# A two-layer attention trunk: 1/rms at the turns through Ln and Exp on ScalarE, and constants in two loads

## Chip, cores and metric

One core of one Trainium2 chip runs the kernel. The metric is the device time of one execution in microseconds (us), smaller is better. Engines are called as in the profile: PE is TensorE (PEld its weight loads), DVE is VectorE, ACT is ScalarE, POOL is GpSimd, SP is SyncE, which issues the DMAs.

## What is computed

Two layers over x of 256 tokens by 1024 channels, f32. Each layer has a token mixer (native sparse attention and block-sparse attention side by side) and a SwiGLU block; each of the two starts with an RMS norm whose scale and shift come from a conditioning vector c. Cut to what matters here:

```python
def rms_norm(x, g, eps=1e-6):
    x32 = x.astype(jnp.float32)
    y = x32 * lax.rsqrt(jnp.mean(x32 * x32, axis=-1, keepdims=True) + eps)
    return y.astype(x.dtype) * g

for l in range(2):
    ada = jax.nn.silu(c) @ w_ada[l] + b_ada[l]
    sh_m, sc_m, g_m, sh_f, sc_f, g_f = jnp.split(ada[:, None, :], 6, axis=-1)
    h = rms_norm(x, norm_mix[l]) * (1.0 + sc_m) + sh_m
    ... = jnp.split(h @ w_in[l], split_at, axis=-1)        # q, k, v, gates
    ...                                                    # both attentions
    x = x + g_m * (merged @ w_out[l])
    h = rms_norm(x, norm_ffn[l]) * (1.0 + sc_f) + sh_f
    gt, up = jnp.split(h @ w_ffn_in[l], 2, axis=-1)
    x = x + g_f * ((jax.nn.silu(gt) * up) @ w_ffn_out[l])
```

## The kernel before

Tokens lie in two tiles of 128 rows (t = 0, 1). A product x·W in f32 is made of three faster passes: x and W are each split into a rounded part `hi` and a rest `lo` (`split_unit`, L665: `hi` is an ACT copy, `lo` a DVE subtraction), and `mm3` issues hi·hi, hi·lo, lo·hi. Weights come through `dma` (L462) into a few `raw` slots of 1 MB; a slot is free again when its `lo` is done. In the lead-in four of the eight blocks of w_in are multiplied whole in f32 (`WHOLE`, tiles `raw,hd`) and four split.

The order of instructions on every engine is written by a planner (`Program.order`, L232). It walks in time over a cost for each operation, gives an operation with several possible engines to the one that ends first after adding `BIAS` (L130), takes the operation with the highest rank when several are ready, and emits one fixed stream for each engine. On the chip each engine follows its stream and waits where an operand is late. A change of one cost or one bias can therefore change the order everywhere. `R.ahead()` and `R.boost` raise a rank.

There are four norms, three of them between two sub-layers, called turns below: turn A after layer 0's mixer (stage `0wout`, L1359), turn B after layer 0's SwiGLU (stage `0fout`, L1430), turn C after layer 1's mixer. The first norm belongs to the lead-in (`lead_in`, L886). At a turn, for each t: `resid` (L1375) multiplies the product by the gate and adds it to x (DVE, two halves), `h_rstd` (L723) sums the squares of the halves (tile `tmp<-x`, ACT L729 or DVE L731), adds the two sums (`ssx`, DVE), makes sum/D + eps (`rx`, DVE L405), and raises it to -1/2 on POOL (L720); `h_norm` (L737) scales x by it (ACT L741, DVE L742); then PE transposes four blocks at a time (L454, `ident,tmp`), and `h_chain_` applies scale and shift and splits into `hp`, which PE multiplies next. PE has matmuls of the other tile to do meanwhile: the products of t = 1 while t = 0 is normed (`OUT_TURNS`), and the next sub-layer's for t = 0 while t = 1 is normed.

In the lead-in SP issues c, x, then for each block k of w_ada a load `sa` and one of w_in `raw`; one load of constants, `vecs` (128 rows of 707 numbers), comes behind block 0. It holds norm gains, b_ada, the compression offsets, the positions, the rope frequencies `inv` and the head gains. DVE adds 1 to some of it (`vecs<-vecs`, L405), makes block 0's scale and shift (`mod_m`) from `sa` and `vecs`, ACT makes `hd` from it, and PE starts on `raw,hd`. `angles` (L858) makes the rope angles out of positions and `inv` by 13 small operations on POOL, then two sines on ACT (`sincos`) with more POOL work between them.

Of the kernel before, what the change touches and what calls it, by code (L numbers as in the profile page):

```python
# [11 lines left out]
AF = mybir.ActivationFunctionType  # L12
# [4 lines left out]
P = 128  # L17
# [82 lines left out]
def AP(x):  # L100
    return x.ap() if isinstance(x, Ref) else x
# [9 lines left out]
class Op:  # L111
    def __init__(self, no, alts, key):
        self.no, self.alts, self.key = no, alts, key
        self.preds, self.succs, self.acc, self.new = {}, [], [], []
        self.bytes = 0
        self.level = 0.0
        self.stage, self.first, self.boost = None, False, 0.0

    def rank(self, e):
        return self.level + self.boost + (FIRST if self.first and e != "PE" else 0.0)  # L120
# [1 line left out]

FIRST = 1000.0
LAT = {"PE": 0.24, "DVE": 0.09, "ACT": 0.09, "POOL": 0.2, "SP": 0.0, "Q": 0.0}
SIZE = {F32: 4, F32R: 4, BF16: 2, I32: 4}


class Program:
    WAIT = 1.0
    BIAS = {"DVE": 0.6, "POOL": 0.5}  # L130

    def __init__(self, nc):
        self.nc, self.ops, self.kinds, self.key, self.open, self.allvals = nc, [], {}, 0.0, None, []
# [98 lines left out]
    def order(self):  # L232
# [13 lines left out]
        out = []  # L246
        eps = {"PE": 0.08, "DVE": 0.05, "ACT": 0.05, "POOL": 0.05, "SP": 0.0, "Q": 0.0}
        ends = {}

        def place(op):  # L250
            t = 0.0
# [29 lines left out]
        while len(out) < len(self.ops):  # L281
            best = None
            per = {}
            while loads and loads[0] in issued:
                loads.popleft()
            for op in ready:
                if "SP" in op.alts and op.no != loads[0] and self.ops[loads[0]].stage == "lead":
                    continue
                pl = place(op)
                if pl is None:  # L290
                    continue
                for e, (c, _) in op.alts.items():
                    est = max(free[e], pl[0],
                              max((f if q == e else f + LAT[q] for f, q in rt[op.no].values()), default=0.0))
                    per.setdefault(e, []).append((est, op, pl[1], c))
            self.done, self.ready = out, ready
            assert per, "stuck"
            for e, cs in per.items():
                t0 = min(c[0] for c in cs)
                if e == "SP":  # L300
                    pick = min(cs, key=lambda c: (max(c[0], free[e] + 0.3), c[1].no))
                else:
                    pick = max((c for c in cs if c[0] <= t0 + eps[e]), key=lambda c: (c[1].rank(e), -c[1].no))
                    if pick[3] > 1.0 and e != "PE":

                        soon = [c for c in cs if c[0] < t0 + self.WAIT * pick[3]
                                and c[1].rank(e) > pick[1].rank(e) + 5.0]
                        if soon:
                            pick = min(soon, key=lambda c: (c[0], -c[1].rank(e)))
                if best is None or pick[0] < best[0]:  # L310
                    best = (pick[0], e, pick[1], pick[2], pick[3])
            t, e, op, picks, c = best
            if len(op.alts) > 1:

                done = {x: next(y[0] for y in per[x] if y[1] is op) + op.alts[x][0] for x in op.alts}
                e = min(done, key=lambda x: done[x] + self.BIAS.get(x, 0.0))
                c = op.alts[e][0]
                t = done[e] - c
            for v, s in zip(op.new, picks):
                v.kind.queue.popleft()  # L320
                v.slot, v.placed = s, True
                for cell in s.cells:
                    cell.busy = True
            if op.bytes:
                free[e] = t + c
                if e == "SP":
                    dma = max(dma, t + c + 0.5) + op.bytes / 385e3
                    end = dma + 2.0
                else:
                    end = t + c + 6.5  # L330
            else:
                free[e] = t + c
                end = t + c
            ends[op.no] = end
            for v in op.acc:
                v.left -= 1
                v.end = max(v.end, end + LAT[e])
                if v.left == 0:
                    for cell in v.slot.cells:
                        cell.busy, cell.free_at = False, v.end  # L340
            ready.remove(op)
            if e == "SP":
                issued.add(op.no)
            for s in op.succs:
                npred[s.no] -= 1
                rt[s.no][op.no] = (end, e if not op.bytes else "SP")
                if not npred[s.no]:
                    ready.append(s)
            out.append((t, e, op))
# [13 lines left out]
class Engines:  # L363
# [52 lines left out]
    def recip(self, out, a):  # L416
        self._vec(("DVE",), cols(out), True, lambda v: v.reciprocal(AP(out), AP(a)), [a], [out])

    def act(self, out, a, func, scale=None, bias=None, accum=None):
        kw, reads = {}, [a]  # L420
        c = (0.17 if self._psum(a) else 0.215) + cols(out) / 1200
        if scale is not None:
# [8 lines left out]
        if accum is not None:  # L431
            kw["accum_out"] = accum
            writes.append(accum)
            c += 0.2
        self.p.op({"ACT": (c, [lambda: self.nc.scalar.activation(AP(out), AP(a), func,  # L435
                                                                 **{k: AP(x) for k, x in kw.items()})])},
                  reads, writes)

    def evac(self, out, a):

# [42 lines left out]
def trunk_kernel(tc, pools, A):  # L483
# [78 lines left out]
    crow = const("crow", [P, D])  # L562
    x = [const(f"x{t}", [P, D]) for t in range(NT)]
    NV = 2 * L * KD + L * 6 * KD + L * 16
    vecs = const("vecs", [P, NV + 35 + 256 * L])
    posi = vecs.of("pos")[:, NV:NV + 3].bitcast(I32)
    inv = vecs.of("inv")[:, NV + 3:NV + 35]
    gvec = [vecs.of("g")[:, NV + 35 + 256 * l:NV + 35 + 256 * (l + 1)] for l in range(L)]
    normT = vecs.of("norm")[:, :2 * L * KD].rearrange("p (a l k) -> p a l k", a=2, l=L)
    bT = vecs.of("b")[:, 2 * L * KD:8 * L * KD].rearrange("p (l s k) -> p l s k", l=L, s=6)  # L570
    peT = vecs.of("pe")[:, 8 * L * KD:NV].rearrange("p (l j) -> p l j", l=L)
# [148 lines left out]
        E_.raw("POOL", 1.1 + 0.13 * n, lambda: nc.gpsimd.tensor_tensor(AP(r), AP(r), AP(mh), op=ALU.pow), [r, mhalf], [r])  # L720
        return r

    def h_rstd(t):  # L723
        xr = [temp(), temp()]
        s2 = small(2, "ssx2")
        ss = small(1, "ssx")
        for i in range(2):
            xi, si, xo = x[t].of(i)[:, i * 512:(i + 1) * 512], s2.of(i)[:, i:i + 1], xr[i]
            R.op({"ACT": (0.84, [(lambda o, a, b: lambda: nc.scalar.activation(AP(o), AP(a), AF.Square, accum_out=AP(b)))  # L729
# [1 line left out]
                  "DVE": (0.77, [(lambda o, a, b: lambda: nc.vector.scalar_tensor_tensor(  # L731
                      AP(o), AP(a), 1.0, AP(a), op0=ALU.mult, op1=ALU.mult, accum_out=AP(b)))(xo, xi, si)])},
                 [xi], [xo, si])
        tt(ss, s2[:, 0:1], s2[:, 1:2], ALU.add)
        return xr, rstd_of(ss, 1, 1.0 / D, EPS, "rx")

    def h_norm(t):  # L737
        xr, r = h_rstd(t)
        for i in range(2):
            xi, xo = x[t].of(i)[:, i * 512:(i + 1) * 512], xr[i]  # L740
            R.op({"ACT": (0.72, [(lambda o, a: lambda: nc.scalar.activation(AP(o), AP(a), AF.Copy, scale=AP(r)))(xo, xi)]),  # L741
# [144 lines left out]
    def lead_in(bs, h, W):  # L886
# [7 lines left out]
        def load(k):  # L894
# [3 lines left out]
            raws[k] = R.val("raw", lambda a: a[:, :NC0])  # L898
            dma(raws[k], W[k * P:(k + 1) * P, :NC0])

        load(0)
        dma(vecs, A["vecs"])
        for k in range(1, KD):
            load(k)
        with R.ahead():
            consts()
# [8 lines left out]
            act(crow.of(i)[:, i * 512:(i + 1) * 512], b, AF.Copy)  # L915
        for kind in (1, 4):
            ts(bT[:, :, kind], bT[:, :, kind], 1.0, None, ALU.add)
        xr = [h_norm(t) for t in range(NT)]
        xT = {}
        for q in range(4):  # L920
            b = R.val("s" if q < 2 else "t")
# [44 lines left out]
    def sublayer_mix(l, h):  # L966
# [397 lines left out]
        for kh in range(2):  # L1364
            for c in range(2):
                us[(c, kh)] = load_unit(WO[kh * 512:(kh + 1) * 512, c * 512:(c + 1) * 512], 4, 512, spare=True)
        for c, kh, t in OUT_TURNS:
            part(bs[(c, t)], mT[t], us[(c, kh)], 4 * kh, kh == 0, kh == 1)
        for t in range(NT):
# [15 lines left out]
    def sublayer_ffn(l, h):  # L1385
# [60 lines left out]
        for i, t, k, c in keys:  # L1446
            kk = 2 * i + k
            cs_ = slice(c * 512, (c + 1) * 512)
            mm3(bs[(t, c)], aT[t][kk], us[i].hi[:, k, cs_], us[i].lo[:, k, cs_], kk == 0, kk == KF - 1)
        hn = []  # L1450
        for t in range(NT):
            for c in range(2):
                resid(l, t, c, bs[(t, c)], ada[l]["g_f"])
# [58 lines left out]
```

## Time and profile before

| what | value |
|---|---|
| median of 3 runs | 848.64 us (848.53 to 852.99) |
| the profiled execution | 847.45 us, its span 845.70 us |
| granted TensorE clock over the span | 0.987 of full speed |
| DMA | 183.82 MB, mean 217 GB/s |
| `vecs` load | 353.5 KB, 8.9 us from issue to landing |
| chain that ended last, by engine | PE 80%, DVE 6%, DMA 6%, ACT 3%, issue 2%, POOL 1% |

The span is the time from the first to the last instruction of the profiled execution; the 1.75 us beside it lie around them. The chain that ended last is followed back from the last instruction, at each step to what released it. A row of the timeline gives start, length, engine, line, operation, out<-in, and in brackets how long the engine had stood idle and what ended it.

### The profile page before, as it was taken

How to read it: one execution, taken by the hardware profiler on the slowest of the kernel's cores; microseconds unless marked ns; L12 is line 12 of the kernel's file. 1: busy time of each engine (PE TensorE's matmuls, PEld its weight loads, DVE VectorE, ACT ScalarE, POOL GpSimd, SP SyncE). 2: the span in 40 equal slices, each digit the busy share in tenths (PEclk: the TensorE clock that was granted, in tenths of full speed). 3: DMA queues.
4: the chain of work that ended last, by engine and by line, in shares of the span. 5: the costliest groups of instructions: out<-in, count | busy, mean ns of one | idle time of the engine just before them, and what ended most of it. 6: DMA issues, size and time to landing. Idle time of an engine off the chain costs nothing.

```text
span 845.7 us, 10445 instructions
## 1 busy us (share of the span) xinstructions
PE 806.8 (95%) x3948; PEld 613.3 (73%) x3948; DVE 578.7 (68%) x1023; ACT 404.2 (48%) x640; POOL 73.7 (9%) x75
## 2 busy tenths in 40 slices
PE   6998999998989999999999879999999999999996
PEld 3666756763778887888878758766567788889885
DVE  7979777766896867776788878674477454365443
ACT  6345275751572444433474345677356533354331
POOL 5411600000010000000012213000001000000000
PEclk9998999999999999999999989999999999999999
DMA  9988364458958888888847765430373455446431
GB/s 362 401 294 285 126 205 165 137 194 312 335 198 291 270 326 306 303 295 332 322 149 218 279 208 190 140 110 1 100 265 133 130 213 198 157 153 245 154 144 50
DMA packets 75204, 183.82 MB, mean 217 GB/s; under 512 B 4113, under 2 KB 9233, under 8 KB 75154
## 3 DMA queue, kind: packets, MB, share of 16 engines
q1 hardware_dynamic: 75154, 183.16, 61.5%
q8 instruction: 31, 0.51, 0.2%
q14 instruction: 19, 0.16, 0.1%
HBM read 182.10 MB, written 1.05 MB: 217 GB/s over the span
## 4 chain that ended last, share of the span: by engine, by line
PE 80%; DVE 6%; DMA 6%; ACT 3%; issue 2%; POOL 1%; POOLq 0%; SPq 0%; DVEq 0%; ACTq 0%
PE bank L450 75%; PE bank L454 5%; DVE lo L387 2%; ACT hi L435 2%; DMA aw<-in_w_ada 1%; DVE tmp L387 1%; DMA raw<-in_w_out 1%; DMA vecs<-in_vecs 1%; DMA raw<-in_w_ffn_in 1%; POOL rx L720 1%; DMA raw<-in_w_in 1%; DVE x L387 1%; DVE aw L393 1%; POOL tmp L387 0%; DVE tmp L405 0%
## 5 line engine op out<-in xcount | busy, mean ns | idle before, releaser
L450 PE MATMUL bank<-hi,hp 128*128 128x512 f32 (+2 forms) x1296 | 408.0, 388 | 4.7 <-DVE tmp L387 2.4
L435 ACT ACTIVATE hi<-raw 128x2048 fp32r<-128x2048 f32 (+2 forms) x107 | 201.5, 1892 | 267.8 <-PE bank L450 204.5
L387 DVE TENSOR_TENSOR lo<-raw,hi 128x2048 fp32r<-128x2048 f32 (+2 forms) x107 | 240.4, 2266 | 126.7 <-ACT hi L435 125.6
L450 PEld LDWEIGHTS bank<-hi,hp 128*128 128x128 f32 x1296 | 240.7, 190 | 60.5 <-issue 5.9
L450 PE MATMUL bank<-lo,hp 128*128 128x512 f32 (+2 forms) x648 | 246.1, 380 | 2.5 <-DVE lo L387 2.5
L450 PEld LDWEIGHTS bank<-lo,hp 128*128 128x128 f32 x648 | 123.3, 190 | 27.7 <-DVE lo L387 3.9
L393 DVE SCALAR_TENSOR_TENSOR aw<-aw,crow 128x1024 f32<-128x1024 f32 x80 | 95.6, 1219 | 24.6 <-DMA aw<-in_w_ada 24.5
L450 PE MATMUL bank<-hi,aT 128*128 128x512 f32 x352 | 111.0, 391 | 0.0
L450 PEld LDWEIGHTS bank<-hi,aT 128*128 128x128 f32 x352 | 66.1, 188 | 13.4
L450 PE MATMUL bank<-lo,aT 128*128 128x512 f32 x176 | 68.7, 390 | 0.0
L450 PE MATMUL bank<-raw,yy 128*128 128x512 f32 x128 | 58.6, 598 | 2.7 <-DVE tmp L393 2.6
L450 PE MATMUL bank<-raw,hd 128*128 128x512 f32 (+1 forms) x112 | 51.1, 586 | 2.0 <-ACT hd L435 2.0
L720 POOL TENSOR_TENSOR rx<-rx,mhalf 128x1 f32<-128x1 f32 x8 | 12.3, 1536 | 466.9 <-DVE rx L405 463.1
L454 PE MATMUL bank<-ident,tmp 128*128 128x128 f32 x256 | 38.8, 284 | 8.0 <-ACT tmp L741 4.2
L454 PEld LDWEIGHTS bank<-ident,tmp 128*128 128x128 f32 x256 | 31.0, 146 | 19.1 <-ACT tmp L741 6.4
L399 DVE CUSTOM_DVE_ANT_0 at<-bank,maskf 128x128 f32<-128x128 f32 (+1 forms) x96 | 29.6, 352 | 22.0 <-PE bank L454 14.6
L450 PE MATMUL bank<-hi,mT 128*128 128x512 f32 x128 | 42.7, 402 | 0.0
L450 PEld LDWEIGHTS bank<-raw,yy 128*128 128x128 f32 x128 | 23.0, 190 | 26.9 <-issue 24.3
L450 PEld LDWEIGHTS bank<-lo,aT 128*128 128x128 f32 x176 | 33.1, 188 | 6.8 <-DVE lo L387 0.2
L435 ACT ACTIVATE at<-at,nb,rqa 128x128 f32<-128x128 f32 (+1 forms) x64 | 34.2, 536 | 4.3 <-DVE nb L393 4.3
L450 PEld LDWEIGHTS bank<-raw,hd 128*128 128x128 f32 x112 | 20.9, 196 | 19.5 <-issue 15.4
L435 ACT ACTIVATE tmp<-bank 128x512 f32<-128x512 f32 (+2 forms) x46 | 22.2, 519 | 18.9 <-PE bank L450 9.0
(172 smaller groups left out, 712.2 us busy)
## 6 DMA issues: line engine op xcount, KB each, us to landing
raw<-in_w_ffn_in SPq DMA_DIRECT2D x44, 1024.0 KB, 6.8
aw<-in_w_ada SPq DMA_DIRECT2D x80, 512.0 KB, 5.4
raw<-in_w_in SPq DMA_DIRECT2D x30, 1024.0 KB, 5.3
raw<-in_w_ffn_out SPq DMA_DIRECT2D x22, 1024.0 KB, 5.0
sa<-in_w_ada SPq DMA_DIRECT2D x8, 1024.0 KB, 10.5
raw<-in_w_out SPq DMA_DIRECT2D x8, 1024.0 KB, 6.1
raw<-in_w_in SPq DMA_DIRECT2D x8, 908.0 KB, 8.4
raw<-in_w_up_nsa SPq DMA_DIRECT2D x4, 1024.0 KB, 5.0
```

The lines of the kernel that those rows point to most:

```text
L387: self._vec(engs, cols(out), True, lambda v: v.tensor_tensor(AP(out), AP(a), AP(b), op=op), [a, b], [out])
L393: lambda v: v.scalar_tensor_tensor(AP(out), AP(a), AP(s), AP(b), op0=op0, op1=op1, **{k: AP(x) for k, x in kw.items()}),
L399: lambda v: v.tensor_tensor_reduce(AP(out), AP(a), AP(b), 1.0, init, op0, op1, AP(accum)),
L435: self.p.op({"ACT": (c, [lambda: self.nc.scalar.activation(AP(out), AP(a), func, **{k: AP(x) for k, x in kw.items()})])}, reads, writes)
L450: self.p.op({"PE": (cost, [lambda: self.nc.tensor.matmul(AP(out), AP(lhsT), AP(rhs), start=start, stop=stop)])}, [lhsT, rhs], [out])
L454: self.p.op({"PE": (0.109, [lambda: self.nc.tensor.transpose(AP(out), AP(a), AP(ident))])}, [a, ident], [out])
L720: E_.raw("POOL", 1.1 + 0.13 * n, lambda: nc.gpsimd.tensor_tensor(AP(r), AP(r), AP(mh), op=ALU.pow), [r, mhalf], [r])
```

## The change

Three edits. At the turns, 1/rms is exp(-ln(sum/D + eps)/2): `ts` makes b = sum of the first half/D + eps as soon as that half is there, ACT does Ln(sum of the second half/D + b) and Exp(-0.5 ·), and the DVE add, the second DVE step and the POOL power go. The lead-in keeps POOL's power but also loses one DVE step. `log_soon` puts a load of ACT's table with both functions ahead of each turn, at a rank above all others, free to go once the last gates (turns A and C) or the last SwiGLU piece (turn B) are written. The planner is told of table loads (1.28 each), and DVE's bias goes from 0.6 to 0.8. `vecs` (now 163 numbers a row) goes ahead of block 0's loads; `rows` (544 a row, `inv` and the head gains) follows block 1.

```diff
-    BIAS = {"DVE": 0.6, "POOL": 0.5}
+    BIAS = {"DVE": 0.8, "POOL": 0.5}
...
+            if op.loads is not None:
+                table = op.loads
+            if e == "ACT" and op.func is not None and op.func not in table:
+                table = next(x for x in TABLES if op.func in x)
+                t = max(t, free[e] + 1.28)
...
-    def h_rstd(t):
+    def h_rstd(t, log):
...
-        ss = small(1, "ssx")
+        b, r = small(1, "ssx"), small(1, "rx")
...
-        tt(ss, s2[:, 0:1], s2[:, 1:2], ALU.add)
-        return xr, rstd_of(ss, 1, 1.0 / D, EPS, "rx")
+            if i == 0:
+                ts(b, si, 1.0 / D, EPS, ALU.mult, ALU.add)
+        s1 = s2.of(1)[:, 1:2]
+        if log:
+            act(r, s1, AF.Ln, scale=1.0 / D, bias=b)
+            act(r, r, AF.Exp, scale=-0.5)
+        else:
+            ts(r, s1, 1.0 / D, b, ALU.mult, ALU.add)
+            E_.raw("POOL", 1.23, lambda: nc.gpsimd.tensor_tensor(AP(r), AP(r), AP(mhalf), op=ALU.pow), [r, mhalf], [r])
+        return xr, r
+
+    def log_soon(late):
+
+        R.boost = 1000.0
+        op = R.op({"ACT": (1.28, [lambda: nc.scalar.preload_act_table_set("natural_log_exp_and_others")])}, late, [])
+        op.loads = TABLES[3]
+        R.boost = 0.0
...
+        dma(vecs, A["vecs"])
         load(0)
-        dma(vecs, A["vecs"])
-        for k in range(1, KD):
+        load(1)
+        dma(rows, A["rows"])
+        for k in range(2, KD):
             load(k)
...
-        xr = [h_norm(t) for t in range(NT)]
+        xr = [h_norm(t, False) for t in range(NT)]
...
+        log_soon([yv, *tgv.values()])
         for c, kh, t in OUT_TURNS:
...
+        if l < L - 1:
+            log_soon(last)
```

## Rows read from the trace of the kernel before

**Rows 1.** Windows: width, busy us (count) of PE, PEld, DVE, ACT, POOL; clock.

```profile
15.00:55.00 40.00, 40.00 (x137) 25.02 (x136) 33.12 (x58) 15.75 (x23) 15.21 (x19) 0.96 0.92 362
224.00:248.00 24.00, 21.53 (x107) 17.40 (x105) 21.32 (x38) 14.81 (x26) 3.99 (x2) 1.00 0.57 196
425.00:443.00 18.00, 16.21 (x84) 12.28 (x83) 14.98 (x26) 13.38 (x24) 4.07 (x2) 1.00 0.40 129
636.00:660.00 24.00, 21.79 (x108) 17.64 (x107) 17.11 (x29) 16.11 (x30) 3.08 (x2) 1.00 0.39 132
```

**Rows 2.** Timeline of turn A: start us, us, engine, instruction, [idle before, releaser].

```profile
241.91 0.74 PE L450 MATMUL bank<-hi,hp 128*128 128x512 f32 x2 [0.84 <-DVE hp L387]
...
242.07 0.19 ACT L729 ACTIVATION_READ_ACCUMULATOR tmp<-x 128x1 f32 x1
...
242.79 2.53 POOL L720 TENSOR_TENSOR rx<-rx,mhalf 128x1 f32<-128x1 f32 x1 [9.27 <-DVE rx L405]
...
245.36 1.34 ACT L741 ACTIVATE tmp<-x,rx 128x512 f32<-128x512 f32 x2 [1.29 <-POOL rx L720]
...
246.14 0.66 PE L454 MATMUL bank<-ident,tmp 128*128 128x128 f32 x4 [1.62 <-ACT tmp L741]
```

**Rows 3.** Timeline of turn B, same columns.

```profile
426.55 0.19 ACT L729 ACTIVATION_READ_ACCUMULATOR tmp<-x 128x1 f32 x1
...
427.20 2.52 POOL L720 TENSOR_TENSOR rx<-rx,mhalf 128x1 f32<-128x1 f32 x1 [181.88 <-DVE rx L405]
...
429.75 1.34 ACT L741 ACTIVATE tmp<-x,rx 128x512 f32<-128x512 f32 x2 [1.73 <-POOL rx L720]
...
430.53 1.27 PE L454 MATMUL bank<-ident,tmp 128*128 128x128 f32 x8 [0.97 <-ACT tmp L741]
```

**Rows 4.** Timeline of turn C, same columns.

```profile
642.91 0.55 POOL L720 TENSOR_TENSOR rx<-rx,mhalf 128x1 f32<-128x1 f32 x1 [126.51 <-DVE rx L405]
...
656.73 0.66 PE L454 MATMUL bank<-ident,tmp 128*128 128x128 f32 x4 [1.62 <-ACT tmp L741]
```

**Rows 5.** Groups by line on ACT: count, busy us, mean ns, idle.

```profile
L435 ACT ACTIVATE hp<-bank,mod_f 128x128 fp32r<-128x128 f32 x8 | 3.4, 450 | 2.6 <-DVE tmp L405 2.6
...
L435 ACT ACTIVATE gates<-bank 128x24 f32<-128x24 f32 x4 | 0.8, 194 | 0.0
```

**Rows 6.** Timeline of ACT: a table load and its successor; ends of idle stretches.

```profile
204.20 1.91 ACT L435 ACTIVATE hi<-raw 128x2048 fp32r<-128x2048 f32 x1 [17.21 <-DMA raw<-in_w_out]
...
250.52 1.28 ACT L435 ACT_TABLE_LOAD   x1
...
251.82 0.60 ACT L435 ACTIVATE tmp<-bank 128x512 f32<-128x512 f32 x1
...
413.79 1.92 ACT L435 ACTIVATE hi<-raw 128x2048 fp32r<-128x2048 f32 x1 [5.78 <-PE bank L450]
...
449.40 1.92 ACT L435 ACTIVATE hi<-raw 128x2048 fp32r<-128x2048 f32 x1 [3.13 <-PE bank L450]
...
614.11 1.91 ACT L435 ACTIVATE hi<-raw 128x2048 fp32r<-128x2048 f32 x1 [8.82 <-DMA raw<-in_w_out]
```

**Rows 7.** Timeline of the lead-in, same columns as turn A.

```profile
11.90 0.25 DVE L405 TENSOR_SCALAR vecs<-vecs 128x16 f32<-128x16 f32 x2 [1.20 <-DMA vecs<-in_vecs]
...
14.45 8.05 PE L450 MATMUL bank<-raw,hd 128*128 128x512 f32 x16 [2.04 <-ACT hd L435]
...
16.65 1.72 ACT L435 ACTIVATE hi<-raw 128x1816 fp32r<-128x1816 f32 x1 [1.80 <-DMA raw<-in_w_in]
...
24.11 0.28 ACT L435 ACTIVATE sincos<-tmp 128x96 f32<-128x96 f32 x1 [3.51 <-POOL tmp L405]
...
29.50 2.04 DVE L387 TENSOR_TENSOR lo<-raw,hi 128x1816 fp32r<-128x1816 f32 x1
...
32.12 0.40 PE L450 MATMUL bank<-lo,hp 128*128 128x512 f32 x1
```

**Rows 8.** Who waited for whom, PE from 443 to 636 us: total, times, longest.

```profile
PE bank L454 <- POOL tmp L387: 3.2, 1, 3.2
```

More of the change, by code (lines that the diff above doesn't have):

```diff
@@ L117, in __init__ @@
         self.stage, self.first, self.boost = None, False, 0.0
+        self.func, self.loads = None, None
     def rank(self, e):
@@ L124 @@
 LAT = {"PE": 0.24, "DVE": 0.09, "ACT": 0.09, "POOL": 0.2, "SP": 0.0, "Q": 0.0}
+TABLES = ((AF.Exp, AF.Tanh), (AF.Sin,), (AF.Silu, AF.Sin, AF.Tanh), (AF.Ln, AF.Exp))
 SIZE = {F32: 4, F32R: 4, BF16: 2, I32: 4}
@@ L248, in order @@
         ends = {}
+        table = ()
         def place(op):
@@ L417, in recip, with act @@
         self._vec(("DVE",), cols(out), True, lambda v: v.reciprocal(AP(out), AP(a)), [a], [out])
-    def act(self, out, a, func, scale=None, bias=None, accum=None):
+    def act(self, out, a, func, scale=None, bias=None, accum=None, late=()):
         kw, reads = {}, [a]
@@ L434, in act @@
             c += 0.2
-        self.p.op({"ACT": (c, [lambda: self.nc.scalar.activation(AP(out), AP(a), func,
-                                                                 **{k: AP(x) for k, x in kw.items()})])},
-                  reads, writes)
+        op = self.p.op({"ACT": (c, [lambda: self.nc.scalar.activation(AP(out), AP(a), func,
+                                                                      **{k: AP(x) for k, x in kw.items()})])},
+                       reads + list(late), writes)
+        if any(func in x for x in TABLES):
+            op.func = func
     def evac(self, out, a):
@@ L564, in trunk_kernel @@
     NV = 2 * L * KD + L * 6 * KD + L * 16
-    vecs = const("vecs", [P, NV + 35 + 256 * L])
+    vecs = const("vecs", [P, NV + 3])
+    rows = const("rows", [P, 32 + 256 * L])
     posi = vecs.of("pos")[:, NV:NV + 3].bitcast(I32)
-    inv = vecs.of("inv")[:, NV + 3:NV + 35]
-    gvec = [vecs.of("g")[:, NV + 35 + 256 * l:NV + 35 + 256 * (l + 1)] for l in range(L)]
+    inv = rows.of("inv")[:, :32]
+    gvec = [rows.of("g")[:, 32 + 256 * l:32 + 256 * (l + 1)] for l in range(L)]
     normT = vecs.of("norm")[:, :2 * L * KD].rearrange("p (a l k) -> p a l k", a=2, l=L)
@@ L733, in h_rstd, with h_norm @@
                  [xi], [xo, si])
[L734 to L738 removed]
+            if i == 0:
[13 more added lines that the diff above has]
+        R.boost = 0.0
+    def h_norm(t, log=True):
+        xr, r = h_rstd(t, log)
         for i in range(2):
@@ L1497 @@
     rows = np.concatenate([np.array(INV_FREQ, np.float32), gains.reshape(-1)])
-    host["vecs"] = np.concatenate([host["vecs"], spots.view(np.float32), np.repeat(rows[None], P, axis=0)], axis=1)
+    host["vecs"] = np.concatenate([host["vecs"], spots.view(np.float32)], axis=1)
+    host["rows"] = np.repeat(rows[None], P, axis=0)
     arrays, aps = {}, {}
```

## The prediction

> **What bounds the kernel now.** I read the page's busy times first: PE is busy nearly all the time, so a change gains only where PE stands still. The view of PE's waits and the windows by stage say where that is. In the lead-in PE stands until its first product of x starts at 14.45, and then runs without a gap from 15 to 55 [rows 1, 7]. The two big products after turns A and C run almost without a gap too. At the turns it stands: the windows show 24.00 - 21.53 = 2.47 us at turn A, 18.00 - 16.21 = 1.79 at B and 24.00 - 21.79 = 2.21 at C, 6.47 in all, at a granted clock of 1.00, the 2.4 GHz level [rows 1]. The chain of waits passes POOL's power in each turn. The rest, some waits in the two mixers and the tail, is touched only by a new order.
>
> The timelines show what ends each gap. At A's second tile the last sum of squares is there at 242.07 + 0.19 = 242.26, POOL's power runs from 242.79 for 2.53, ACT scales x at 245.36, and PE starts its transposes at 246.14 after standing 1.62 [rows 2]. At C the same gap is 1.62 [rows 4]. At B it is the first tile: sum at 426.74, POOL 427.20 for 2.52, ACT at 429.75, PE after 0.97 [rows 3]. So three gaps, 4.21 us, hang on the power. The power itself took 0.55 once [rows 4] and 2.52 to 2.53 where it stood beside a long DVE subtraction [rows 2, 3]: most of it is waiting, not arithmetic. The remaining 6.47 - 4.21 = 2.26 are later steps of the same chain: 0.85 at A behind a `hp` rest on DVE [rows 1, 2], 0.82 at B and 0.59 at C.
>
> **The turns.** From the last sum to the scaling it takes 3.10 us at A [rows 2] and 3.01 at B [rows 3]; this goes, with its three hand-overs between engines. In its place stand Ln and Exp of one column on ACT, which made the sum. No row has them. Bounds: a small activation without operand pointers took 194 ns, one of 128 columns with two pointers 450 [rows 5]. Ln has one pointer (b), Exp none, so both together cost 0.39 to 0.90; I take 0.5, nearer the 24-column row. b waits for DVE only by a step made while ACT squares the second half. So the chain shrinks by about 2.5, more than each gap, and the three close: 1.62 + 0.97 + 1.62 = 4.21. Below that they can stay open only if ACT is busy with something else (a rival). What is late next is the 2.26: the same `hp` chain arrives earlier, but DVE's residual adds for the other tile and the block-by-block hand-overs stay, and at C the first tile's power took only 0.55, so there is little to win. I take somewhat under half, 1.0 (bounds 0 and 2.26). The turns' sum is 5.2 (4.2 to 6.5). PE's matmuls afterwards follow without a gap, so a gain at a turn is kept.
>
> On ACT the edit adds Ln, Exp and table loads. A load took 1.28, and the next activation started 0.02 behind it [rows 6]. Three preloads are new; Silu was loaded after the turns already. Behind turn B the gates' Tanh of layer 1 now needs a load that it didn't need, and the load for Exp later in that layer goes. So the net is three loads, 3.85 us of ACT. I cost them at nothing, because ACT stood idle 17.21, 5.78 and 8.82 us just ahead of the turns and 3.13 behind the gates [rows 6]. Without that cover they cost up to 3.85.
>
> **The lead-in.** The wait of DVE for `vecs` was 1.20, and its two adds of 0.25 stood behind that [rows 7]; both were ahead of the step that makes `hd`, which ended PE's wait. With `vecs` first they are done before block 0 lands. Against that, 353.5 x 163/707 = 81.5 KB go ahead of block 0, some 0.25 us at the pace of the DMA in that stretch. PE starts 1.2 earlier. The moved DMA is one more issue of SP ahead of block 0, hidden by the 1 MB of x in flight.
>
> What it costs: `rows` lies behind block 1, so the bytes up to its end are those that stood up to the end of block 1's `raw` before, and that was there when ACT split it at 16.65 [rows 7]. The rope frequencies arrive 4.75 later than at 11.90. The 13 POOL steps then ended at 24.11, where ACT had stood 3.51 for them: 12.2 from the landing. If they take that again, ACT stands until 28.9, and the split of the fourth block queues behind it on ACT. Its rest on DVE began at 29.50 and ended at 31.54; PE's first use of a rest after that is at 32.12 [rows 7], so the slack is 0.58. A block of w_in also gets its slot from it, so a delay goes on to the end of the lead-in. Worst: the whole 4.75 goes on to that rest, and it ends 4.75 - 0.58 = 4.2 behind PE's use. Best: POOL runs faster, and all of the 1.2 stays. Between -1.2 and +4.2 I take 0: POOL's steps were long where DVE worked, and DVE soon stands idle when ACT does, so POOL should make up most of it; a point just over the middle of the worse side, 2.4, is a rival.
>
> The row behind that is the power's 0.55 against 2.53. The Trainium skill ("SBUF — State Buffer", "SBUF: two separate sides") says that DVE with two SBUF inputs and POOL exclude each other on a shared pair of ports for a whole instruction. By that rule the delay on POOL is DVE's work, in the lead-in too; the rows agree.
>
> **The order.** BIAS 0.8 moves work from DVE to ACT or POOL, and every engine's order is new. Its mean I take as 0. The nearest price is a residual: one add on POOL held PE for 3.2 [rows 8].
>
> **The sum.** On the profiled execution 847.45 - 5.2 = 842.2 (of it 1.75 outside the span). The median of the runs lies 1.19 above that execution, so the forecast is 848.64 - 5.2 = 843.4.
>
> **The rivals.**
> 1. The lead-in gains as well: everything closes, 848.64 - 6.47 - 1.2 = 841.0. For it: PE ran without a gap in the lead-in. Against: the slack of 0.58.
> 2. The rope angles block ACT: 848.64 - 5.2 + 2.4 = 845.8. For it: ACT already stood 3.51 there, and the landing moves by 4.75. Against: POOL's speed when DVE is idle. The Trainium skill's rule of the shared ports, named above, speaks for it.
> 3. The table loads come out on the path: 848.64 - 5.2 + 3.85 = 847.3. Against: the idle stretches [rows 6]. The Trainium skill ("ScalarE: Activation LUTs", "What ACT_TABLE_LOAD costs") has 2.66 us for a switch with its drain; by that figure the three would cost 8.0 and the time be 851.4. The row's 0.02 behind the load speaks against the drain.
> 4. The change doesn't do what it says: Ln waits on ACT behind a split of 1.9 at each turn. Then the chain is 2.4 instead of 3.1, it wins 0.7 at each of the three gaps, and the time is 848.64 - 2.1 = 846.5. For it: a split followed the square directly at A and C. Against: the turn's chain has the higher rank.
> 5. Slower: the higher bias puts more adds ahead of transposes on POOL, where a DVE subtraction holds them. At 3.2 each [rows 8] the gain of 5.2 is used up from the second on: two give 849.8, three 853.0. For it: this happened once. Against: the add costs POOL more in the plan than DVE even with 0.2 added.
>
> **How the numbers follow.** The measurement can tell 0.5%, 4.2 us, from no change: faster is below 844.4, slower above 852.9. Chances: the forecast 0.50 with its own range 841.5 to 846, rival 1 0.13, rival 2 0.18, rival 3 0.05, rival 4 0.05, rival 5 0.09. Below 844.4 lie four fifths of the forecast's half and all of rival 1: 0.53. Above 852.9 lies rival 5 with three adds or with rival 2 on top: 0.06. The rest, 0.41, is the same. The range of 8 in 10 goes from 840.2, just under rival 1, to 849.3, over rivals 2 to 4.
>
> **What would show it.** Right: PE's gaps of 1.62, 0.97 and 1.62 ahead of the transposes are gone, Ln and Exp stand directly behind the last square and take about 0.5, and the three preloads lie in ACT's idle stretches. In the lead-in PE starts near 13.2. `sincos` shows rival 2: if ACT stands for POOL beyond 27 and PE waits behind it for a DVE `lo`, the 1.2 is gone. Wrong would be gaps at the turns that only change their releaser, or new waits of PE in the mixers for POOL or DVE.

## The result, and the profile after

Measured in alternation with the kernel before, 20 executions of each, the changed kernel took 845.92 us (median; 842.91 to 849.25) against 850.61 (846.32 to 854.43): a ratio of 0.9948 with a 95% interval of 0.9933 to 0.9964, faster by 4.7 us. The forecast was 843.4 with a range from 840.2 to 849.3. So sign and time came out as forecast, but the sum behind them did not: the turns gave about a fifth of what was counted on them, and in the two profiles a term that I had set to zero gave the rest.

Executions of one kernel differ by several us, and the profiled one of after (848.27 us, span 846.5) is a long one, that of before (847.45, span 845.7) a short one. Their spans can't be set against each other. What can is TensorE's (PE's) idle time: span less PE's busy time. Of before it is 845.7 - 806.84 = 38.9 us, of after 846.5 - 811.88 = 34.6: less by 4.3, about what the medians say. The other side, the 5.0 us by which PE was busy longer with the same 3948 instructions, belongs to the one execution.

The windows of the kernel after (width, busy us and count of PE, PEld, DVE, ACT, POOL; clock, DMA share, GB/s). The first three are the turns; each begins 3 us ahead of the turn's first residual and is 24 us wide, which for the kernel before shows the same 2.47, 1.79 and 2.21 as [rows 1]. The last is the whole execution:

```profile
227.80:251.80 24.00, 22.63 (x108) 17.38 (x106) 20.84 (x35) 19.83 (x36) 0.00 (x0) 1.00 0.57 186
420.30:444.30 24.00, 20.83 (x95) 16.05 (x94) 19.30 (x36) 17.63 (x37) 0.00 (x0) 0.93 0.41 132
639.60:663.60 24.00, 23.14 (x110) 18.11 (x109) 18.17 (x30) 19.85 (x36) 0.00 (x0) 1.00 0.30 97
0.00:847.00 847.00, 811.88 (x3948) 615.95 (x3948) 576.18 (x1008) 418.29 (x668) 64.72 (x69) 0.99 0.62 217
```

POOL is gone from the turns. PE idles 1.37 at A, 3.17 at B and 0.86 at C: 5.40 us where it was 6.47. The turns gave 1.07, not 5.2. Outside the turns PE idles 34.6 - 5.4 = 29.2 us where it was 38.9 - 6.5 = 32.4: 3.2 us came from there.

Turn A's second tile, timeline of the kernel after (start us, us, engine, instruction, [idle before, releaser]), to be read beside [rows 2]:

```profile
243.97 0.19 ACT L741 ACTIVATION_READ_ACCUMULATOR tmp<-x 128x1 f32 x1
244.19 0.29 ACT L444 ACTIVATE rx<-ssx,ssx 128x1 f32<-128x1 f32 x1
...
244.52 0.20 ACT L444 ACTIVATE rx<-rx 128x1 f32<-128x1 f32 x1
244.75 1.34 ACT L768 ACTIVATE tmp<-x,rx 128x512 f32<-128x512 f32 x2
...
245.53 0.66 PE L465 MATMUL bank<-ident,tmp 128*128 128x128 f32 x4 [0.71 <-ACT tmp L768]
```

The chain is what the prediction said: Ln and Exp stand directly behind the last sum, and from the sum (244.16) to the scaling it takes 0.59 us instead of 3.10. But PE still stands 0.71 ahead of the transposes. At C the same gap is 0.73, and at B it is closed. What is left at A comes from PE's side. These are the windows from 3 us ahead of the turn's first residual to the end of PE's work ahead of the gap, in the kernel before and in the kernel after:

```profile
225.25:244.52 19.27, 18.42 (x88) 14.75 (x86) 16.59 (x32) 13.44 (x23) 3.19 (x2) 1.00 0.56 199
```

```profile
227.85:244.82 16.97, 16.81 (x79) 12.90 (x77) 14.15 (x27) 12.91 (x26) 0.00 (x0) 1.00 0.57 196
```

PE gets there 2.30 us sooner in the turn: 1.61 because the new order gives it less to do first (79 matmuls instead of 88), 0.69 because it idled less. The last sum comes 0.70 sooner (16.31 into the window instead of 17.01), and the chain behind it is 2.51 shorter: 1.62 - 0.70 - 2.51 + 2.30 = 0.71.

In place of its gap B has three others:

```profile
434.69 1.28 DVE L396 TENSOR_TENSOR x<-x,tmp 128x512 f32<-128x512 f32 x2
434.92 0.50 PE L461 MATMUL bank<-hi,hp 128*128 128x512 f32 x1 [0.76 <-ACT hp L444]
...
435.90 0.68 DVE L396 TENSOR_TENSOR hp<-tmp,hp 128x512 fp32r<-128x512 f32 x1
...
436.63 1.06 PE L461 MATMUL bank<-hi,hp 128*128 128x512 f32 x2 [0.98 <-DVE ssx L414]
...
441.86 1.31 DVE L396 TENSOR_TENSOR lo<-raw,hi 128x1120 fp32r<-128x1120 f32 x1
...
443.23 0.40 PE L461 MATMUL bank<-lo,hp 128*128 128x280 f32 x1 [1.43 <-DVE lo L396]
```

PE takes up the first tile sooner than before (its transposes start at 429.17, 8.85 into the window, instead of 10.20), uses up its first half, and then waits for the second half: its rest `hp` (435.90) stands on DVE behind the second tile's residual (434.69). The releaser named at 436.63 is the small step that follows `hp` on DVE; the operand is `hp`. The last gap is a `lo` of the weights that stands on DVE behind other work.

Outside the turns, two waits are shorter or gone. In the mixer of layer 0 the kernel before had this (PE's waits from 170 to 224 us: total, times, longest):

```profile
PE bank L450 <- DVE tmp L393: 2.6, 2, 1.7
PE bank L450 <- DVE lo L387: 0.3, 1, 0.3
```

and the kernel after this:

```profile
PE bank L461 <- DVE lo L396: 0.9, 1, 0.9
PE bank L461 <- ACT yy L453: 0.7, 1, 0.7
```

1.3 us less. At the opening of layer 1 the add on POOL of [rows 8] had held PE for 3.16. Three such adds of the rotary step stood on POOL there, and beside that wait the kernel before had these from 444 to 523 us:

```profile
PE bank L450 <- ACT vbd L435: 3.4, 1, 3.4
PE bank L450 <- DVE tmp L387: 2.4, 1, 2.4
```

In the kernel after the three adds are on DVE, and PE's waits in the same stretch are, but for one of 0.2,

```profile
PE bank L461 <- DVE tmp L396: 2.1, 1, 2.1
PE bank L461 <- ACT vbd L444: 1.7, 1, 1.7
PE bank L465 <- DVE kbd_tok L414: 1.5, 1, 1.5
PE bank L461 <- DVE lo L396: 1.4, 1, 1.4
```

7.07 us of idle time in that stretch where it was 9.06: 2.0 less. The wait for POOL went and the one for `vbd` halved, but two new waits for DVE took back 2.9. So 1.07 + 1.3 + 2.0 = 4.4 us account for the 4.3.

That is one pair of profiles. Of the kernels below, same_order and same_order2 have PE's old order and power_back the new one. From 150 us to turn A, where PE idled 2.85 before and 1.57 after, they show 2.14 and 2.66 against 1.74; in the 79 us behind turn B, 9.06 twice against 8.00. So the two shares are better read as 0.4 to 1.3 and 1.1 to 2.0.

### The profile page after: what moved, and what is told of

Read it like the earlier page. It is cut to its first block, busy times and chain, and to the rows that moved or that the text cites. A ratio compares the mean times of both kernels' runs of the same rounds, so it can differ in the third digit from the quotient of the medians.

```text
span 846.5 us, 10445 instructions
## 1 busy us (share of the span) xinstructions
PE 811.9 (96%) x3948; PEld 615.9 (73%) x3948; DVE 576.2 (68%) x1008; ACT 418.3 (49%) x668; POOL 64.7 (8%) x69
## 4 chain that ended last, share of the span: by engine, by line
PE 78%; DVE 8%; DMA 6%; ACT 4%; POOL 2%; issue 1%; SPq 0%; DVEq 0%; POOLq 0%; ACTq 0%
PE bank L461 73%; PE bank L465 5%; DVE lo L396 4%; DMA raw<-in_w_out 2%; ACT hi L444 2%; DMA rows<-in_rows 2%; DMA aw<-in_w_ada 1%; DVE tmp L396 1%; DMA raw<-in_w_ffn_in 1%; POOL tmp L396 1%; POOL tmp L414 1%; DVE tmp L414 1%; ACT hp L444 1%; DMA raw<-in_w_in 1%; DVE x L396 0%
## 5 line engine op out<-in xcount | busy, mean ns | idle before, releaser
L461 PE MATMUL bank<-lo,hp 128*128 128x512 f32 (+1 forms) x648 | 246.7, 381 | 4.6 <-DVE lo L396 4.5
L461 PEld LDWEIGHTS bank<-lo,aT 128*128 128x128 f32 x176 | 33.1, 188 | 6.7 <-DVE lo L396 0.2
L453 ACT ACTIVATE pt<-bank 128x512 f32<-128x512 f32 x35 | 20.8, 594 | 21.7 <-PE bank L465 21.7
L732 POOL TENSOR_TENSOR r<-r,mhalf 128x4 f32<-128x4 f32 x4 | 4.1, 1020 | 355.0 <-DVE r L414 355.0
```

The source lines that it names most:

```text
L453: self.p.op({"ACT": (0.17 + n / 1200, [lambda: self.nc.scalar.activation(AP(out), AP(a), AF.Copy)]), "DVE": (0.155 + n / 960, [lambda: sel ...
L461: self.p.op({"PE": (cost, [lambda: self.nc.tensor.matmul(AP(out), AP(lhsT), AP(rhs), start=start, stop=stop)])}, [lhsT, rhs], [out])
```

## The experiments

Theory one was the prediction's: the power in the turns costs what its three gaps show, and its removal brings that, in any order of the rest. Theory two: the gain needs the order that the planner makes for the changed kernel. All twelve kernels were timed in alternation with the kernel before. The table has PE's idle time from each profile and the ratio of times; the idle time leaves out what an execution takes longer in the same instructions.

| kernel | turns A + B + C | elsewhere | PE idle | ratio to before, 95% |
|---|---|---|---|---|
| before | 2.47 + 1.79 + 2.21 = 6.5 | 32.4 | 38.9 | |
| after | 1.37 + 3.17 + 0.86 = 5.4 | 29.2 | 34.6 | 0.9948 [0.9933, 0.9964] |
| same_order | 1.91 + 1.28 + 2.21 = 5.4 | 33.4 | 38.8 | 0.9992 [0.9968, 1.0016] |
| same_order2 | 1.75 + 1.23 + 1.71 = 4.7 | 35.3 | 40.0 | 0.9977 [0.9953, 1.0000] |
| turns_only | 1.39 + 2.98 + 0.87 = 5.2 | 36.5 | 41.8 | 1.0037 [1.0007, 1.0066] |
| loads_only | 2.48 + 1.80 + 2.27 = 6.6 | 33.9 | 40.4 | 1.0030 [1.0005, 1.0056] |
| bias_only | 2.57 + 1.80 + 2.22 = 6.6 | 33.1 | 39.7 | 1.0031 [1.0006, 1.0055] |
| loads_bias | 2.47 + 1.78 + 2.24 = 6.5 | 35.6 | 42.1 | 1.0040 [1.0016, 1.0065] |
| old_bias (turns, loads) | 1.39 + 2.99 + 1.13 = 5.5 | 32.8 | 38.3 | 1.0007 [0.9981, 1.0032] |
| no_loads (turns, bias) | 1.39 + 3.16 + 0.88 = 5.4 | 32.4 | 37.8 | 0.9976 [0.9956, 0.9996] |
| power_back | 4.71 + 5.17 + 4.69 = 14.6 | 30.2 | 44.8 | 1.0107 [1.0064, 1.0150] |
| vecs_behind | 1.33 + 3.18 + 0.87 = 5.4 | 37.6 | 42.9 | 1.0096 [1.0071, 1.0120] |
| bias7 | 1.31 + 2.99 + 0.88 = 5.2 | 30.9 | 36.1 | 0.9981 [0.9957, 1.0005] |
| tile0 | 2.47 + 3.22 + 1.84 = 7.5 | 30.0 | 37.5 | 0.9983 [0.9956, 1.0009] |

**same_order: the power away, the order kept.** Ln and Exp are issued behind the last square; the plan keeps the power's steps, with nothing issued for them, so that PE and SP run exactly the streams of before. A table preload is issued ahead of each turn, as in the change.

```diff
+        def tail():
+            ...
+            nc.vector.tensor_scalar(b, a[:, 0:1], 1.0 / D, EPS, op0=ALU.mult, op1=ALU.add)
+            nc.scalar.activation(AP(r), a[:, 1:2], AF.Ln, scale=1.0 / D, bias=b)
+            nc.scalar.activation(AP(r), AP(r), AF.Exp, scale=-0.5)
...
+        R.op({"POOL": (1.23, [lambda: None])}, [r, mhalf], [r])
```

> The kernel before with the power at the turns replaced by Ln and Exp on ACT (b on DVE, table preloads as in the change), while the planner still counts DVE's two steps and POOL's power: the streams of PE and SP stay instruction for instruction those of before. Theory 1 (the power's chain holds PE at the turns): PE's gaps of 1.62, 0.97 and 1.62 ahead of the transposes close, the later gaps of 2.26 stay for the most part, 3.5 to 4.5 us less than before. Theory 2 (the gain needs the new order, the chain is covered or waits for something else as soon as the power is gone): under 1.5 us less.

It gained nothing that can be told: 0.9992, and 1.07 us in the turns, as its second theory had it. Its turn A shows why:

```profile
239.82 0.18 ACT L742 ACTIVATION_READ_ACCUMULATOR tmp<-x 128x1 f32 x1
...
240.37 0.20 ACT L738 ACTIVATE rx<-rx 128x1 f32<-128x1 f32 x1
...
240.48 1.90 ACT L435 ACTIVATE hi<-raw 128x2048 fp32r<-128x2048 f32 x1
...
242.28 1.32 ACT L763 ACTIVATE tmp<-x,rx 128x512 f32<-128x512 f32 x2
243.04 0.66 PE L454 MATMUL bank<-ident,tmp 128*128 128x128 f32 x4 [0.62 <-ACT tmp L763]
```

The exponential is done at 240.57, but the scaling comes at 242.28: between them stands a split of 1.90, which in the kernel before had filled ACT's wait for the power. The planner had covered most of the power with it. Once the power is gone, the cover is the delay. The three gaps still fell to 0.62, 0 and 0.89, but PE's waits for the first tile's `hp`, 0.84 at A and 0.58 at C before, grew to 1.30 and 1.31.

**same_order2: the split out of the way.** The scaling of each tile's first half is issued behind the exponential:

```diff
             nc.scalar.activation(AP(r), AP(r), AF.Exp, scale=-0.5)
+            nc.scalar.activation(AP(xr[0]), AP(x[t].of(0)[:, :512]), AF.Copy, scale=AP(r))
```

> As same_order (TensorE's and SyncE's streams are those of the kernel before, the power is gone, logarithm and exponential stand on ScalarE), but the scaling of each tile's first half is issued on ScalarE directly behind the exponential, ahead of the evacuation (the split's first part, 1.9 us) that stood between the two in same_order. Theory one (rows 2 to 4: the three gaps of 1.62, 0.97 and 1.62 us hang on the way from the last sum of squares to the scaling, wherever the order comes from): the gaps close, TensorE idles some 4 us less in the three turns than in the kernel before, and the time falls by 3 to 4 us, ratio 0.995 to 0.997. Theory two (the gain needs the new order): the split that is now 0.7 us later holds TensorE as much as the scaling did before it, the turns keep an idle time of 5 us or more, and the ratio is 0.998 to 1.001.

The ratio was 0.9977, on the edge between the two. Turn A:

```profile
233.94 3.70 ACT L435 ACTIVATE hi<-raw 128x2048 fp32r<-128x2048 f32 x2
...
237.54 0.44 ACT L435 ACTIVATE hp<-bank,mod_f 128x128 fp32r<-128x128 f32 x1
...
243.69 0.73 PE L450 MATMUL bank<-hi,hp 128*128 128x512 f32 x2 [1.49 <-DVE hp L387]
...
244.46 0.72 ACT L739 ACTIVATE tmp<-x,rx 128x512 f32<-128x512 f32 x1
...
247.65 0.55 PE L454 MATMUL bank<-ident,tmp 128*128 128x128 f32 x3 [0.26 <-ACT tmp L768]
```

The three gaps of the power are now 0.26, 0 and 0.26 (1.62, 0.97 and 1.62 before): theory one was right on those, 3.7 of 4.2 us. But the wait for `hp` grew at A from 0.84 to 1.49 and at C from 0.58 to 1.45. That `hp` is the first tile's and stands ahead of the second tile's gap. At A the split that had filled ACT's wait for the first tile's power now runs behind the scaling, two splits in a row (233.94), and the first tile's evacuation starts 0.36 later than before: 8.10 us behind the turn's first residual (229.44) instead of 7.74. That is part of the 0.65. The work that covered one wait comes back in another. The turns kept 4.7 us, a net gain of 1.8, and the time fell by about 2.0 (0.9977). Its profile shows 2.9 us more idle time elsewhere, with PE's stream unchanged; the times don't show that, so single profiles scatter by that much outside the turns.

**Each part alone, and two at a time.** turns_only has the power replaced and the preloads in the plan, with the old load and the old preference of 0.6 for VectorE; loads_only and bias_only are the kernel before with that part; old_bias, no_loads and loads_bias leave one part out of the change. The edits are those of the change's diff, for instance

```diff
-    BIAS = {"DVE": 0.8, "POOL": 0.5}
+    BIAS = {"DVE": 0.6, "POOL": 0.5}
```

> The change's turns, preloads and planner rules, with the one load of constants and DVE's bias of 0.6 of before. Theory 1: the turns are the whole gain, 4 to 6 us less than before, as much as the whole change or a little more. Theory 2: less than 2.5 us, since the bias and the loads would bring the rest.

> The kernel before with only the constants in two loads, the small one ahead of block 0. Theory of the forecast: PE's first product about 1.2 us earlier, the rope angles later, together 0 (from -1.2 to +4.2). Rival, from the profile after the change (first product only 0.13 earlier, the compression products 2.5 later): the load ahead of block 0 delays block 0 by as much as it saves, and the kernel is 1 to 2.5 us slower than before.

> The kernel before with only DVE's bias at 0.8. Theory 1: a new order of mean 0, within 2 us of before. Theory 2: the bias takes work off DVE in the mixers and brings 2 us or more.

> The whole change but for the planner's preference for VectorE, which stays at 0.6: logarithm and exponential, table preloads, two loads. If the gain of the whole change is that of the turns' power (theory one), about 0.995 like the kernel after; if it comes only with the order that the higher preference gives (theory two), 1.000 to 1.005, as turns_only and loads_only gave.

> The whole change but for the loads: the constants come in one load behind w_ada's first block, as in the kernel before. Theory one: 0.995 or a little lower, since the two loads alone cost 0.3%. Theory two, in the form that the turns' gain needs the preference of 0.8: 0.995 too; in the form that it needs the loads as well: 1.000 to 1.004.

> The kernel before with the two loads and the preference of 0.8, and the power still on GpSimd in the turns: all of the change but its turns. Theory one: no gain, 1.000 to 1.006 (the two parts alone gave 1.003 each), so that the difference to the kernel after, some 0.8%, is what the turns give within this order. Theory two in its strongest form (the gain is one of order, not of the turns): 0.995 to 0.997.

Each part alone made the kernel slower by 0.3 to 0.4%, loads and bias together by 0.4%, all three together faster by 0.5%. Neither theory of turns_only had a loss in it, and the 2.6 us that bias_only lost lie outside both of its theories, though its interval reaches into the first. The 2.6 us of loads_only are what its rival said, but not for the rival's reason, since PE's first product started 0.33 earlier there (14.12). loads_bias came out by its first theory, old_bias by its second, and no_loads between its two. The parts don't add: the same turns are worth +0.4% on the kernel before, and -0.9% on loads_bias (0.9948 against 1.0040). The turns themselves can't be the reason, since of these kernels all with the change's turns idle 5.2 to 5.5 us there and all with the old ones 6.5 to 6.6. The difference lies elsewhere, from 29.2 to 36.5 us. Two waits in it can be tied to parts. PE's wait for the add on POOL at the opening of layer 1 is in all kernels whose plan has the power in the turns (before, same_order, same_order2, loads_only, bias_only, loads_bias: 3.2 each time) and in none whose plan has the logarithm. The wait in the mixer of layer 0 (2.6 in before) is 2.6 in turns_only, 2.3 in old_bias, 1.3 in no_loads, and gone where logarithm, two loads and a preference of 0.7 or more come together (after, bias7, tile0, power_back, vecs_behind). Of the 4.1 that turns_only lost elsewhere, 2.3 stand ahead of 100 us and the rest is spread. Why the planner's order comes out so was not followed further.

**bias7: half the preference.**

```diff
-    BIAS = {"DVE": 0.8, "POOL": 0.5}
+    BIAS = {"DVE": 0.7, "POOL": 0.5}
```

> The whole change with a preference for VectorE of 0.7, half way from 0.6 (1.0007) to 0.8 (0.9948). If the preference itself gives the gain, step by step: 0.997 to 0.999. If the orders are draws that share only the turns: the turns idle 5.2 to 5.6 us as in all kernels with the change's turns, and the ratio is anywhere from 0.995 to 1.002, following the idle time outside the turns.

0.9981, between 1.0007 (0.6) and 0.9948 (0.8), with the turns unchanged at 5.2. Three points in order speak for the first expectation; since the intervals of neighbours touch, the second isn't excluded.

**power_back: the order of after, with the power in it.** The reverse of same_order: the plan is that of the change, and its two steps issue VectorE's multiply-add and GpSimd's power. No table is preloaded in the turns.

```diff
-            act(r, s1, AF.Ln, scale=1.0 / D, bias=b)
-            act(r, r, AF.Exp, scale=-0.5)
+            # the plan's two steps on ScalarE issue the power's two steps
+            for step, func, kw in (
+                    (lambda: nc.vector.tensor_scalar(AP(r), AP(s1), 1.0 / D, AP(b), op0=ALU.mult, op1=ALU.add),
+                     AF.Ln, dict(a=s1, scale=1.0 / D, bias=b)),
+                    (lambda: nc.gpsimd.tensor_tensor(AP(r), AP(r), AP(mhalf), op=ALU.pow),
+                     AF.Exp, dict(a=r, scale=-0.5))):
+                act(r, func=func, **kw)
+                R.ops[-1].alts["ACT"] = (R.ops[-1].alts["ACT"][0], [step])
```

> The kernel after with its own order on every engine, but the two steps of the logarithm and the exponential issue the power again (VectorE's multiply and add, then GpSimd's power), and no table is preloaded in the turns. TensorE's and SyncE's streams are those of the kernel after. The three turns idle 5.4 us in the kernel after, 6.5 in the one before. Theory one (the gain of the whole change is mainly that of order elsewhere, since the turns differ by 1.1 us only): the ratio stays at 0.996 to 0.997, turns at 6.5 to 7. Theory two (the order of the kernel after leaves no work between the last sum of squares and the scaling, so that the power, back in it, is uncovered): scalings come 1.5 to 2.5 us later each, the turns idle 9 to 12 us, and the ratio is 0.999 to 1.003.

Theory two held here, and more strongly than expected: 1.0107, 1.6% above the kernel after, and 14.6 us of idle time in the turns, 9.2 more. Turn A, second tile:

```profile
242.36 2.29 DVE L396 TENSOR_TENSOR lo<-raw,hi 128x2048 fp32r<-128x2048 f32 x1
...
244.56 0.21 DVE L752 TENSOR_SCALAR rx<-ssx,ssx 128x1 f32<-128x1 f32 x1
244.85 0.55 POOL L754 TENSOR_TENSOR rx<-rx,mhalf 128x1 f32<-128x1 f32 x1 [10.61 <-DVE rx L752]
...
245.44 1.34 ACT L774 ACTIVATE tmp<-x,rx 128x512 f32<-128x512 f32 x2 [2.88 <-POOL rx L754]
...
246.21 1.57 PE L465 MATMUL bank<-ident,tmp 128*128 128x128 f32 x8 [3.01 <-ACT tmp L774]
```

The same subtraction in the kernel before, beside its power of 2.53 (242.79) [rows 2], as the first of two:

```profile
242.63 4.48 DVE L387 TENSOR_TENSOR lo<-raw,hi 128x2048 fp32r<-128x2048 f32 x2
```

The power takes 0.55 here, not 2.53, and from the last sum to the scaling it is 2.88 all the same, where it was 3.10 in the kernel before: the multiply-add ahead of the power stands on DVE behind the subtraction of 2.29. So at this tile the delay is that subtraction in both kernels. In the kernel before ACT had a split in that time and PE other matmuls; here ACT stands 2.88 and PE 3.01. Part of the 9.2 is the place where DVE's step was put, and it is no pure price of the power; but it is what two more hand-overs cost in an order that leaves them no room. Outside the turns it idles 30.2, close to the 29.2 of after, without the preloads: they cost nothing there that can be seen.

**vecs_behind: the small load behind block 0.**

```diff
-        dma(vecs, A["vecs"])
         load(0)
+        dma(vecs, A["vecs"])
         load(1)
```

> The whole change, but the small load stands behind the loads of block 0 and ahead of those of block 1. If the 81 KB ahead are what made block 0's w_ada part land 1.3 us later, it lands at some 9 us again, and VectorE waits for the small load instead, about 1 us, as in the kernel before; TensorE's first product then stays at 14.1 to 14.5 us and the time at 0.993 to 0.996, as the kernel after. If the planner's order, which the moved load shifts in 98 places of TensorE's stream, decides more than the load: 0.997 to 1.002, with the turns' idle time unchanged at 5.4 us.

1.0096, far off both expectations. Lead-in of vecs_behind, timeline and window:

```profile
11.01 0.25 DVE L414 TENSOR_SCALAR vecs<-vecs 128x16 f32<-128x16 f32 x2 [2.71 <-DMA vecs<-in_vecs]
...
13.19 1.22 DVE L402 SCALAR_TENSOR_TENSOR sa<-sa,crow 128x1024 f32<-128x1024 f32 x1
...
18.02 2.93 PE L461 MATMUL bank<-raw,hd 128*128 128x512 f32 x3 [5.48 <-ACT hd L444]
```

```profile
15.00:55.00 40.00, 36.57 (x120) 22.25 (x121) 30.36 (x57) 14.77 (x23) 16.80 (x22) 1.00 0.77 294
```

With the load behind block 0 the plan puts the adds on `vecs` ahead of the first dot product on DVE, so DVE stands 2.71 for them and the dot product, 10.20 in after, comes at 13.19; PE's first product comes at 18.02. Then the loads fall behind too (294 GB/s from 15 to 55 us), PE has gaps where it had none, and up to 100 us it idles 8 us more than in after. So what costs here is the place of the adds in DVE's order. In no_loads, where the one load also lies behind block 0, the dot product stands ahead of the adds on DVE, and PE's first product starts at 14.62. What the small load ahead is worth by itself this run doesn't show.

**tile0: the first tile ahead of the second.** An attempt at a better kernel: the first tile's chain gets a higher rank, to close the gaps that turn B now has.

```diff
-HBOOST = (20.0, 20.0)
+HBOOST = (40.0, 20.0)
```

> The whole change, with the first tile's chain ranked ahead of the second tile's (20 more) in the turns, so that in turn B the second tile's residual no longer stands on VectorE between the two halves of the first tile's evacuation (0.76 and 0.98 us of TensorE's idle time in the kernel after). Theory one: those 1.7 us close, the turns idle 3.5 to 4.5 us instead of 5.4, and the ratio is 0.992 to 0.994. Theory two (order elsewhere moves as well, 178 places of TensorE's stream): turn B's idle time falls, but the ratio is 0.995 to 1.001. Rival within the turn: the second tile is now late, and its wait takes over the 1.7 us.

The rival within the turn came true. PE's waits ahead of the second tile's transposes at A, and then two of its waits at B:

```profile
242.43 0.66 PE L465 MATMUL bank<-ident,tmp 128*128 128x128 f32 x4 [1.82 <-ACT tmp L768]
```

```profile
433.13 0.74 PE L461 MATMUL bank<-hi,hp 128*128 128x512 f32 x2 [0.38 <-DVE hp L396]
439.23 0.39 PE L461 MATMUL bank<-lo,hp 128*128 128x280 f32 x1 [1.99 <-DVE lo L396]
```

At B 0.98 became 0.38, and 1.43 became 1.99; at A and C the second tile waits 1.82 and 1.84 instead of 0.71 and 0.73. The turns idle 7.5 us, and nothing is won. No kernel of these is faster than the kernel after.

## Why the prediction was right or wrong

- **What bounds the kernel.** Right in sign: of the thirteen changed kernels only same_order2 (1.2 us more idle, 0.2% faster) and old_bias (0.6 less, 0.1% slower) have a ratio that doesn't go with PE's idle time. In size the two can differ: power_back and vecs_behind are 9.1 and 8.2 us slower than the kernel before with 5.9 and 4.1 more idle, and the rest of that isn't explained.
- **The chain of the turns.** Right to the number: Ln and Exp took 0.29 and 0.20 (forecast 0.5 together), and the chain shrank from 3.10 to 0.59, by 2.51 (forecast 2.5).
- **"More than each gap, and the three close: 4.21."** This step failed. Of the three gaps 0.71, 0 and 0.73 are left, so 2.77 closed. I read a gap as the amount by which the chain was late, in an order that stays, and took it that only other work on ACT could keep it open. In the kernel after ACT has none there, but PE reaches the gap sooner, at A with 1.61 us less work ahead of it. same_order and same_order2 show that an order that stays doesn't help either: work that had filled the wait now delays the chain (1.90 of a split) or the first tile's `hp`.
- **"What is late next ... 1.0 of 2.26."** The term that was mis-sized most. The later waits didn't shrink by 1.0 but grew from 2.26 to 5.40 - 1.44 = 3.96, by 1.7: from 0.82 to 3.17 at B, while A and C gave back 0.6. At B I had looked only at the first tile. Its bounds of 0 and 2.26 excluded a loss without a reason. The turns' sum is 1.07 instead of 5.2.
- **Table loads at nothing.** Right: preloads stand at 194.42, 419.52 and 606.19, in stretches in which PE doesn't wait for ACT; outside the turns power_back without them idles no less. The load itself, in the kernel after:

```profile
419.52 1.28 ACT L760 ACT_TABLE_LOAD   x1
420.82 1.09 ACT L453 ACTIVATE gbc<-bank 128x512 f32<-128x512 f32 x2
```

  The Trainium skill ("ScalarE: Activation LUTs", "What ACT_TABLE_LOAD costs") gives a switch with its drain 2.66. The trace differs, and it decides: the load takes 1.28 here and the next activation starts 0.02 behind it, as in [rows 6]. Rival 3 doesn't apply.
- **The lead-in at 0.** Right in the sum. Timeline of the kernel after:

```profile
7.07 0.25 DVE L414 TENSOR_SCALAR vecs<-vecs 128x16 f32<-128x16 f32 x2 [0.37 <-DMA vecs<-in_vecs]
...
10.20 1.23 DVE L402 SCALAR_TENSOR_TENSOR sa<-sa,crow 128x1024 f32<-128x1024 f32 x1 [1.02 <-DMA sa<-in_w_ada]
...
14.32 6.33 PE L461 MATMUL bank<-raw,hd 128*128 128x512 f32 x8 [1.62 <-ACT hd L444]
```

```profile
15.00:55.00 40.00, 39.94 (x132) 24.28 (x130) 32.06 (x55) 15.47 (x22) 17.60 (x22) 1.00 0.98 370
```

  `vecs` no longer holds DVE, but block 0 is 1.33 later in this profile (10.20 instead of 8.87) where I had 0.25 from the bytes, so PE starts 0.13 earlier here, not 1.2. This pair of profiles misleads. Over all profiles in which DVE waits for it, block 0 lands at 9.39 to 10.20 with the small load ahead (five, median 9.56) and at 8.87 to 10.21 without (five, median 9.04): by the medians some 0.5 of the 1.33 is the load, an estimate, since the two ranges overlap; the rest is scatter. PE's first product starts at 13.71 to 14.93 in the seven profiles with the small load ahead (median 13.93) and at 14.45 to 15.81 in the six with one load (median 14.95; vecs_behind, with its other order on DVE, left out): 1.0 earlier, near the forecast's 1.2. The sum is 0 all the same: up to 55 us PE idles 6.79 and 6.84 in the median of the same profiles. What it gains at its start it loses in the stretch behind it, where it stands 0.06 to 1.68 with two loads and 0 to 0.81 with one. ACT's `sincos` ended its wait for POOL near the 28.9 of rival 2,

```profile
28.54 0.28 ACT L444 ACTIVATE sincos<-tmp 128x96 f32<-128x96 f32 x1 [2.04 <-POOL tmp L414]
```

  but in the kernel after PE has next to no gap behind it: 39.94 of 40.00 busy. Rival 1 and rival 2 don't apply.
- **The order at 0.** The other step that failed: in these two profiles it gave 3.2 us, which by chance made up for most of what the turns lacked. The profile of before doesn't hold its size; what the forecast lacked is a width for it. Over eleven different orders of PE "elsewhere" runs from 29.2 to 37.6, so -3 to +5 us around before's 32.4, while with PE's order unchanged it is 32.4, 33.4 and 35.3. I also had the direction of rival 5 wrong in the main: the adds at the opening of layer 1 went from POOL to DVE, and PE's wait of 3.2 went with them, while one new wait of 1.2 for an add on POOL came in layer 0's mixer.
- **Rival 4** (a split of 1.9 in the chain) isn't in the kernel after; it is in same_order, behind the exponential instead of ahead of the logarithm, and there little was gained, as the rival said.
- **Left open.** PE's busy time differs by up to 6 us between profiles with the same instructions (806.8 to 813.0). 1.6 us of that, in the one profile of after, is the clock (below); the rest I can't place.

## What to carry to other kernels

A gap that ends at an engine tells who came last, not what is won by making it faster: look at what the order has put into the wait, and at how much other work the waiting engine has ahead of it. Where a planner orders the work, price the removal of an operation with the order kept, which is a small experiment (here 0.1 and 0.2%, hardly told from nothing), and treat the new order as a term of its own, with a width and not with a mean of zero. Compare profiles by the idle time of the bounding engine when executions scatter as much as the effect.

## What the hardware showed that I had not expected

- The landing of the first block scatters by 0.8 to 1.3 us between profiles with the same loads ahead of it, more than the 0.5 by which 81.5 KB ahead of it moved the median. A difference of one microsecond in the lead-in of two single profiles says nothing.
- GpSimd's power of one column took 0.55 us alone and 2.52 beside a long DVE subtraction [rows 2 to 4]. In power_back five of the six in the turns took 0.54 to 0.55, each right behind such a subtraction instead of beside it, and the one beside a DVE dot product took 1.45. That agrees with the Trainium skill ("SBUF — State Buffer", "SBUF: two separate sides"): DVE with two SBUF inputs and POOL exclude each other on a shared pair of ports.
- After two gaps of 0.76 and 0.98 us within 3 us, PE's granted clock in turn B of after fell. Windows of 2 us:

```profile
434.00:436.00 2.00, 0.89 (x3) 0.30 (x2) 2.00 (x5) 1.43 (x4) 0.00 (x0) 1.00 0.00 0
436.00:438.00 2.00, 1.37 (x4) 1.08 (x5) 2.00 (x5) 1.90 (x8) 0.00 (x0) 0.71 0.00 0
438.00:440.00 2.00, 2.00 (x7) 1.51 (x6) 0.93 (x2) 1.70 (x3) 0.00 (x0) 0.50 0.54 145
```

  0.50 is the level of 1.2 GHz; by the granted shares 2 x 0.29 + 2 x 0.50 = 1.6 us of PE's time went there, an estimate. In turns_only, old_bias and bias7, with 0.58 for the first gap and 0.97 to 0.98 for the second, the clock in the turn was 1.00 throughout, and in no_loads, vecs_behind and power_back too, with 0.75 and 0.98 to 0.99: of seven profiles with much the same gaps one shows the fall.
